# One scheduler flag: the queues of a two-block attention kernel laid by a timeline simulation

## The chip, the cores and the metric

The kernel runs on one core of one Trainium2 chip. The metric is the device time of one execution in microseconds (us). TensorE (PE) multiplies, VectorE (DVE), ScalarE (ACT) and GpSimd (POOL) work elementwise, and SyncE (SP) issues most of the loads. Each engine takes its instructions from a queue of its own, strictly in the order in which they stand there, and waits where an operand or a buffer is not ready.

## What is computed

Two transformer blocks run one after the other on 512 tokens of width 1024, everything in float32. Cut to what matters:

```
mod = silu(c) @ w_ada + b_ada                       # shift, scale, gate
h   = rms_norm(x, g_pre) * (1 + scale) + shift
proj = h @ w_in                                     # qa ka va fa za | qb kb vb zb
oa  = forgetting_attention(qa, ka, va, fa) * silu(za)    # "fox": 8 heads of 64, causal, with decay
ob  = sliding_window_sink_attention(rope(qb), rope(kb), vb) * silu(zb)   # "SWA": 8 query heads, 2 kv heads
x   = x + gate * rms_norm(concat(oa, ob) @ w_out, g_post)

h = rms_norm(x, norm_g);  mem_h = rms_norm(mem, mem_norm_g)
c_glu, c_gate, d_q, d_k, d_v, d_gate, x_q, x_gate, merge = split(h @ w_in_2)
y_conv = conformer_conv(c_glu, c_gate)              # a*sigmoid(b), depthwise convolution with 31 taps, layer norm, projection
y_diff = differential_attention(d_q, d_k, d_v)      # 8 heads, two softmax maps each, p0 - lam * p1, norm, projection
y_mem  = memory_cross_attention(x_q, mem_h)         # 4 heads of 256 over 256 memory tokens, projection
g = sigmoid(merge);  x = x + (g0*y_conv + g1*y_diff + g2*y_mem) @ w_out_2
```

## The kernel before

**Products.** Every float32 operand of a large product is split into a high and a low part; a product is three matmuls, hi·hi, hi·lo and lo·hi. A weight chunk is loaded as `raw` (load_w, the DMA at L164), ACT casts it to `wh` (L169), DVE or POOL subtracts to get `wl` (L171). mm_T (L190) streams 512 tokens per matmul, mm_N (L199) 256 columns. 128x128 transposes are PE instructions too (`tp`).

**Stages.** First come the loads, the memory's keys and values (their normalisation ends in L463 on `mk`) and the modulation: for each of eight chunks of w_ada a product of one row is summed on DVE as scale-and-add steps (gemv, L317 to L320), and its result makes one slice of the normalised input (ada, L366 to L373, `hh` and `hl`). Then the SWA items (scores at L655), then the fox items (scores L735 and L736, softmax L738 to L742, transposes and split causal_tp L751 to L754, values fox_pv L773), then w_out and the norms (finish, with hn at L817 and its transposes at L821), then the differential attention of the second block (scores L1022 and L1023, softmax L1025 to L1032, values L1056), the memory attention (scores L1157), and at the end the three branch projections, the merge and w_out_2. The gate row of the first block (gate_row) is eight more such one-row products, run as filler of the fox items. A tile's name with its number, as sc_3174, stands for one buffer of the program; it is the same tile before and after.

**What sets the order.** An attention stage is a list of items. For each item a helper emits the scores, the values of an earlier item, the transposes of the one before, and then pieces of other work out of a queue of generators (`fill`), a generator's piece being a group of matmuls:

```
    def staged(items, first, second, last, lag, k):
        for i in range(n + lag + 1):
            if i < n:
                first(items[i])
            if i - lag - 1 >= 0:
                last(items[i - lag - 1])
            if 0 <= i - lag < n:
                second(items[i - lag])
            fill(k(i) if callable(k) else k)
```

For the fox items these are the projections that later heads need (qk2, qk3), the gate za1 and the gate row, and after the last item the split of the eight head pairs for w_out, of which the first two take the buffers of the first values:

```
    staged([(pr, m, n) for pr in range(4) for m in range(2) for n in range(NT)], fox_sc, fox_tp, fox_pv, 2, 1)
    o45 = [fa.tile([P, 2, S], F32R, tag=t, name="o45") for t in ("vh0", "vl0")]
```

So no w_out matmul can stand ahead of the last matmul that reads vh0 and vl0 (pv_3395, head pair 1). The convolution's 30 taps per channel tile (L904, after the first at L902) are emitted with a low priority, so that DVE takes them where it has nothing else. All of this is only the order of emission and its priorities: the tile framework then walks through a simulated execution of the program and puts, engine by engine, the ready instruction of the highest priority next into that engine's queue. The queues are fixed before anything runs on the chip.

## Time and profile before

| what | value |
|---|---|
| three runs | 1195.54, 1196.16 and 1196.78 us, median 1196.16 |
| the profiled execution | 1196.61 us, of which the span of the trace is 1194.8 |
| TensorE's mean granted clock in it | 0.991 of full speed |
| busy: PE, DVE, ACT, POOL | 1154.0, 926.6, 551.7, 213.3 us |
| chain of waits that ended last | PE 63%, DVE 24%, issue 3%, ACT 1% of the span |
| moved by DMA | 165.43 MB, 138 GB/s |

"Busy" of PE counts each matmul from its start to a modelled end, and since matmuls are pipelined these overlap: 24 matmuls of 512 columns, each listed with about 0.39 us, start within 5.5 us. What PE has to do is therefore better counted from start to start. A stage below is named by the first score matmul of the item with which it begins; the first start of these on PE is at 131.6 us (sc_1686, the first SWA item), 209.1 (sc_2589, the first fox item), 253.5 (sc_3174), 291.5 (sc_3593), 304.3 (sc_3737, the last fox item), 410.6 (sc_5129, the first differential item), 701.2 (sc_8482, the last), 745.2 (sc_8881, memory attention) and 827.0 (sc_9755).

### The profile page before, as it was taken

Reading aid. Unit: us, or ns where it says so; the run is one execution under the profiler, and the core shown is the slowest. Engines: PE = TensorE matmul, PEld = TensorE weight load, DVE = VectorE, ACT = ScalarE, POOL = GpSimd, SP = SyncE. Lnnn points to the kernel's source line nnn. Section 1 sums busy time; section 2 is a strip of 40 time slices with the busy share of each in tenths; the row PEclk is TensorE's granted clock in tenths of the full one; section 3 lists DMA queues with packets and bytes.
Section 4 is the critical chain, followed back from the end, with each engine's and each line's share of the span. In section 5 each row is a group of like instructions: output and inputs, shape, how many; then the busy total and the mean of one; then the engine's idle time right before and its main releaser. Section 6 shows DMA issues by size and latency. Waiting matters only on the chain.

```text
span 1194.8 us, 18995 instructions
## 1 busy us (share of the span) xinstructions
PE 1154.0 (97%) x6960; PEld 1015.9 (85%) x6960; DVE 926.6 (78%) x2055; ACT 551.7 (46%) x1173; POOL 213.3 (18%) x161
## 2 busy tenths in 40 slices
PE   7879999999989999999999999999999999999998
PEld 6878887878889988998999887988888888888898
DVE  6997777898686699999989999999692596543341
ACT  7646566557554354445554452544422354232230
POOL 1334200000112211120111221221010132011020
PEclk9989999999999999999999999999999999999999
DMA  8765312443463423324233343333446755433232
GB/s 336 259 212 164 105 56 87 152 148 110 150 231 131 124 71 98 106 89 115 89 116 106 124 141 106 106 116 106 152 147 227 267 186 185 132 97 101 86 123 79
DMA packets 61965, 165.43 MB, mean 138 GB/s; under 512 B 7120, under 2 KB 15568, under 8 KB 60848
## 3 DMA queue, kind: packets, MB, share of 16 engines
q1 hardware_dynamic: 36560, 122.41, 32.5%
q10 hardware_dynamic: 25312, 41.82, 10.0%
q8 instruction: 55, 0.90, 0.3%
q14 instruction: 38, 0.31, 0.1%
HBM read 136.80 MB, written 20.58 MB: 132 GB/s over the span
## 4 chain that ended last, share of the span: by engine, by line
PE 63%; DVE 24%; issue 3%; ACT 1%; DMA 0%; POOL 0%; ACTq 0%; DVEq 0%; POOLq 0%
PE mm L190 40%; PE mm L199 15%; DVE cv L904 7%; DVE wl L171 3%; DVE dp L1025 1%; PE pv L773 1%; DVE dp L1032 1%; PE tp L751 1%; DVE dp L1031 1%; DVE ptl L754 1%; PE sc L1157 1%; PE pv L694 1%; PE pv L1200 1%; DVE qs L259 1%; PE tp L266 1%
## 5 line engine op out<-in xcount | busy, mean ns | idle before, releaser
L169 ACT CAST wh<-raw 128x512 fp32r<-128x512 f32 x372 | 215.3, 620 | 217.7 <-PE mm L190 96.2
L171 POOL TENSOR_TENSOR wl<-raw,wh 128x512 fp32r<-128x512 f32 (+1 forms) x93 | 141.8, 1525 | 831.9 <-ACT wh L169 668.8
L171 DVE TENSOR_TENSOR wl<-raw,wh 128x512 fp32r<-128x512 f32 (+1 forms) x279 | 201.7, 747 | 95.3 <-ACT wh L169 94.9
L190 PE MATMUL mm<-hh,wh 128*128 128x512 f32 x640 | 255.9, 400 | 0.0
L190 PE MATMUL mm<-hh,wl 128*128 128x512 f32 x640 | 251.8, 393 | 0.0
L190 PE MATMUL mm<-hl,wh 128*128 128x512 f32 x640 | 251.7, 393 | 0.0
L199 PE MATMUL mm<-wh,hh 128*128 128x256 f32 (+1 forms) x672 | 193.5, 289 | 0.2 <-ACT hh L824 0.2
L904 DVE SCALAR_TENSOR_TENSOR cv<-u,vec,cv 128x512 f32<-128x512 f32 x240 | 191.1, 796 | 3.4
L199 PE MATMUL mm<-wl,hh 128*128 128x256 f32 (+1 forms) x672 | 190.7, 284 | 0.3 <-POOL wl L171 0.3
L199 PE MATMUL mm<-wh,hl 128*128 128x256 f32 (+1 forms) x672 | 190.8, 284 | 0.0
L190 PEld LDWEIGHTS mm<-hh,wl 128*128 128x128 f32 x640 | 120.5, 188 | 27.0
L190 PEld LDWEIGHTS mm<-hh,wh 128*128 128x128 f32 x640 | 120.6, 188 | 24.7
L190 PEld LDWEIGHTS mm<-hl,wh 128*128 128x128 f32 x640 | 120.8, 189 | 24.5
L199 PEld LDWEIGHTS mm<-wl,hh 128*128 128x128 f32 x672 | 128.5, 191 | 0.8 <-POOL wl L171 0.6
L199 PEld LDWEIGHTS mm<-wh,hh 128*128 128x128 f32 x672 | 127.9, 191 | 0.8 <-ACT hh L824 0.5
L199 PEld LDWEIGHTS mm<-wh,hl 128*128 128x128 f32 x672 | 128.3, 191 | 0.0
L190 PE MATMUL mm<-bh,wh 128*128 128x512 f32 x192 | 75.9, 396 | 0.0
L190 PE MATMUL mm<-bh,wl 128*128 128x512 f32 x192 | 75.4, 393 | 0.0
L190 PE MATMUL mm<-bl,wh 128*128 128x512 f32 x192 | 75.4, 393 | 0.0
L1027 ACT ACTIVATE dp<-dp,dst 128x128 f32<-128x128 f32 (+3 forms) x64 | 35.5, 556 | 54.8 <-DVE dst L1025 54.6
L199 PE MATMUL mm<-wl,mh 128*128 128x256 f32 x128 | 39.3, 307 | 6.5 <-DVE wl L171 6.5
L190 PEld LDWEIGHTS mm<-bl,wh 128*128 128x128 f32 x192 | 36.1, 188 | 8.4 <-issue 0.2
(326 smaller groups left out, 2122.4 us busy)
## 6 DMA issues: line engine op xcount, KB each, us to landing
raw<-in_w_dram SPq DMA_DIRECT2D x120, 512.0 KB
raw<-in_w_out_dram SPq DMA_DIRECT2D x24, 512.0 KB
raw<-in_w_mem_dram SPq DMA_DIRECT2D x16, 512.0 KB
ada<-in_w_ada_dram SPq DMA_DIRECT2D x8, 1024.0 KB
ada<-in_w_gate_dram SPq DMA_DIRECT2D x8, 512.0 KB
k<-ks SPq DMA_DIRECT2D x32, 128.0 KB
o_d<-sph ACTq DMA_DIRECT2D x16, 256.0 KB
o_d<-spl ACTq DMA_DIRECT2D x16, 256.0 KB
```

Source lines behind the costliest of these rows:

```text
L169: act.copy(out=wh[:, s], in_=raw[:, s])
L171: eng.tensor_tensor(out=wl[:, s], in0=raw[:, s], in1=f(wh[:, s]), op=ALU.subtract)
L190: m = pe.matmul(out=ps, lhsT=a[:, c0:c0 + P], rhs=at(b, k), start=(n == 0 and i == 0), stop=(n == KT - 1 and i == 2))
L199: pe.matmul(out=ps, lhsT=at(a, k)[:, t * P:(t + 1) * P], rhs=b[:, 0:n], start=(start and m == 0 and i == 0), stop=(stop and m == len(order ...
L259: dve.scalar_tensor_tensor(out=s[b], in0=ps[a], scalar=sc, in1=f(s[a]), op0=ALU.mult, op1=ALU.subtract)
L266: pe.transpose(out=ps[:, t * P:(t + 1) * P], in_=src[:, t, c0:c0 + P], identity=ident)
L694: pe.matmul(out=pv4[0:64], lhsT=l_, rhs=r_[:, j], start=(cnt == 0), stop=(cnt == 3 * nk - 1))
L751: pe.transpose(out=tp[:, j * P:(j + 1) * P], in_=pt_[:, j * P:(j + 1) * P], identity=ident)
L754: dve.tensor_tensor(out=ptl[:, 0:n + 1, n * P:w], in0=tv, in1=f(pth[:, 0:n + 1, n * P:w]), op=ALU.subtract)
L773: pe.matmul(out=pv[0:64, j * P:], lhsT=l_, rhs=r_[:, j, j * P:], start=(j == 0 and i == 0), stop=(j == NT - 1 and i == 2))
L904: dve.scalar_tensor_tensor(out=a, in0=u[:, j:j + S], scalar=dw[:, m * 31 + j:m * 31 + j + 1], in1=a, op0=ALU.mult, op1=ALU.add)
L1027: act.activation(out=p_[:, :w], in_=p_[:, :w], func=AF.Exp, scale=-1.0, bias=st_[:, 0, n, m:m + 1], accum_out=st_[:, 1, n, m:m + 1])
```

## The change

The tile context is told to lay the queues with another simulation of the program, one that takes its times from a timeline model; emission order, priorities, tiles, transfers and arithmetic stay.

```
-    with tile.TileContext(nc) as tc:
+    with tile.TileContext(nc, schedule_with_timeline_sim=True) as tc:
```

Each engine has the same instructions on the same tiles before and after, also the same number of them; only their order in the queues differs. PE's matmuls stand on average 14 places from where they were (at most 124), DVE's instructions 9, ACT's 5, POOL's and SP's about 1. From sc_9755 on, the order is practically that of before.

**First place: PE among the fox items.** The score matmuls of two successive items (L735, L736; sc_3506, sc_3534), before:

```order
L735 MATMUL sc_3506<-k1_3291,qs_3254 128x256
L736 MATMUL sc_3506<-k2_3293,q2_3292 128x256
L751 MATMUL tp_3514<-cst_79,fp_3434 128x128 x4
L190 MATMUL mm_3521<-hh_83,wh_3446 128x512
L190 MATMUL mm_3521<-hl_84,wh_3446 128x512
L190 MATMUL mm_3521<-hh_83,wl_3447 128x512
...
L735 MATMUL sc_3534<-k1_3291,qs_3254 128x384
L736 MATMUL sc_3534<-k2_3293,q2_3292 128x384
```

and now:

```order
L735 MATMUL sc_3474<-k1_3291,qs_3254 128x128
L736 MATMUL sc_3474<-k2_3293,q2_3292 128x128
L751 MATMUL tp_3412<-cst_79,fp_3333 128x128
L735 MATMUL sc_3506<-k1_3291,qs_3254 128x256
L736 MATMUL sc_3506<-k2_3293,q2_3292 128x256
L773 MATMUL pv_3395<-pth_3149,vh_2028 64x512
L735 MATMUL sc_3534<-k1_3291,qs_3254 128x384
L736 MATMUL sc_3534<-k2_3293,q2_3292 128x384
```

Before, twelve projection matmuls (mm_3521, L190) stand between two items. In the new order the last of them stand ahead of sc_3330, six items earlier, and between these items there is nothing but the attention itself. From sc_1686 to sc_3174 there are now 325 matmuls of L190 where there were 224, and from sc_3174 to sc_3593 11 where there were 112.

**Second place: DVE at the last of the eight products for the modulation** (acc_985, whose sum L320 the last slice of hh waits for), before:

```order
L319 SCALAR_TENSOR_TENSOR acc_985<-ada_890,cs_106,acc_985 128x256
L319 SCALAR_TENSOR_TENSOR acc_986<-ada_890,cs_106,acc_986 128x256
L171 TENSOR_TENSOR wl_1128<-raw_1125,wh_1127 128x528
L368 SCALAR_TENSOR_TENSOR mod_188<-sc_976,vec_78 128x2
L320 TENSOR_TENSOR acc_985<-acc_985,acc_986 128x256
```

and now:

```order
L317 TENSOR_SCALAR acc_985<-ada_890,cs_106 128x256
L319 SCALAR_TENSOR_TENSOR acc_986<-ada_890,cs_106,acc_986 128x256
L320 TENSOR_TENSOR acc_965<-acc_965,acc_966 128x256
L369 SCALAR_TENSOR_TENSOR gs_187<-mod_188,vec_78 128x1
L171 TENSOR_TENSOR wl_1314<-raw_1311,wh_1313 128x512
L319 SCALAR_TENSOR_TENSOR acc_985<-ada_890,cs_106,acc_985 128x256
L171 TENSOR_TENSOR wl_1314<-raw_1311,wh_1313 128x512
```

Ahead of the last L320 DVE now has 30 subtractions of L171 where it had 25, and all eight L463, of which it had none there. On SP two chunks of the first projection's weights (w1c) and one of the next stand ahead of the fourth pair of memory weights and of the second pair of x loads (L379, which wait for a buffer).

**Third place: DVE among the differential items** (softmax of the second item of a head: L1025 takes scores and row maximum, L1029 to L1032 normalise; L904 are taps, L210 to L219 a reciprocal root in ten small steps), before:

```order
L217 TENSOR_SCALAR ru_5411<-rt_5410 128x32
L1029 RECIPROCAL drr_5085<-dst_5084 128x2
L904 SCALAR_TENSOR_TENSOR cv_5023<-u_5020,vec_78,cv_5023 128x512
L218 TENSOR_TENSOR rt_5410<-rt_5410,ru_5411 128x32
L1030 TENSOR_TENSOR drr_5085<-drr_5085,nlam_104 128x1
L904 SCALAR_TENSOR_TENSOR cv_5023<-u_5020,vec_78,cv_5023 128x512
L219 SCALAR_TENSOR_TENSOR ry_5409<-rt_5410,ry_5409 128x32
L1031 TENSOR_SCALAR dp_5478<-dp_5478,drr_5085 128x128
```

and now:

```order
L211 TENSOR_SCALAR ry_5409<-rv_5408 128x32
L1029 RECIPROCAL drr_5085<-dst_5084 128x2
L171 TENSOR_TENSOR wl_5739<-raw_5736,wh_5738 128x512
L904 SCALAR_TENSOR_TENSOR cv_5023<-u_5020,vec_78,cv_5023 128x512
L171 TENSOR_TENSOR wl_5739<-raw_5736,wh_5738 128x512
L212 TENSOR_TENSOR rt_5410<-ry_5409 128x32
L1030 TENSOR_TENSOR drr_5085<-drr_5085,nlam_104 128x1
L904 SCALAR_TENSOR_TENSOR cv_5023<-u_5020,vec_78,cv_5023 128x512
```

The small steps of the reciprocal root are spread over a longer stretch and the weight subtractions stand earlier. On PE the transposes of an item (L751) and its values (L1056) now stand behind 10 to 20 matmuls of projections that followed them before.

## Rows read from the trace of the kernel before

**Rows 1.** The page's first part: busy us, share of the span, instructions.
```profile
PE 1154.0 (97%) x6960; PEld 1015.9 (85%) x6960; DVE 926.6 (78%) x2055; ACT 551.7 (46%) x1173; POOL 213.3 (18%) x161
```

**Rows 2.** The chain that ended last, in time order: start, us, what.
```profile
283.91 2.75 PE mm L190 x12
...
417.43 5.75 PE mm L199 x48
...
978.40 166.59 PE mm L190 x720
1144.99 45.96 PE mm L199 x384
```

**Rows 3.** Stages: us; busy PE, PEld, DVE, ACT, POOL (instructions); clock; DMA share, GB/s.
```profile
131.60:209.10 77.50, 76.53 (x459) 64.42 (x459) 60.26 (x187) 49.67 (x136) 9.69 (x12) 1.00 0.23 69
209.10:253.50 44.40, 43.64 (x271) 37.38 (x269) 39.74 (x134) 23.19 (x59) 3.88 (x3) 1.00 0.53 162
253.50:291.50 38.00, 37.41 (x193) 30.24 (x193) 34.36 (x102) 23.23 (x55) 2.82 (x2) 1.00 0.41 125
291.50:304.30 12.80, 12.38 (x92) 11.00 (x91) 12.19 (x40) 10.40 (x27) 1.30 (x1) 1.00 0.18 45
304.30:410.60 106.30, 101.57 (x788) 96.70 (x787) 73.89 (x148) 53.52 (x107) 22.41 (x18) 1.00 0.52 167
410.60:701.20 290.60, 283.23 (x1901) 259.48 (x1901) 281.05 (x691) 140.48 (x318) 49.14 (x29) 1.00 0.34 102
701.20:733.10 31.90, 31.24 (x155) 25.90 (x153) 31.69 (x58) 12.74 (x26) 8.22 (x5) 1.00 0.44 148
733.10:745.20 12.10, 9.57 (x44) 8.11 (x44) 10.85 (x21) 2.71 (x8) 0.00 (x0) 0.86 0.27 91
745.20:827.00 81.80, 81.68 (x506) 72.62 (x505) 76.00 (x133) 39.89 (x84) 18.13 (x12) 1.00 0.33 107
827.00:1194.80 367.80, 363.93 (x1779) 305.06 (x1777) 199.06 (x286) 114.58 (x206) 54.53 (x35) 1.00 0.45 148
```

**Rows 4.** The same view in stretches of 4 us.
```profile
68.00:72.00 4.00, 2.00 (x9) 1.74 (x10) 4.00 (x11) 3.12 (x6) 2.00 (x1) 0.59 0.86 333
72.00:76.00 4.00, 2.22 (x11) 1.93 (x10) 3.90 (x9) 1.80 (x3) 1.55 (x2) 0.50 0.93 367
340.00:344.00 4.00, 2.43 (x22) 2.23 (x21) 3.72 (x10) 3.33 (x8) 1.28 (x1) 1.00 0.98 309
```

**Rows 5.** DVE's groups at 209.1 to 304.3: busy us, mean ns | idle before.
```profile
L319 DVE SCALAR_TENSOR_TENSOR acc<-ada,cs,acc 128x128 f32<-128x128 f32 x48 | 16.5, 377 | 0.0
L738 DVE CUSTOM_DVE_ANT_0 fp<-sc,cst 128x128 f32<-128x128 f32 (+3 forms) x30 | 14.1, 474 | 2.8 <-PE sc L736 2.5
L742 DVE TENSOR_SCALAR fp<-fp,fst 128x128 f32<-128x128 f32 (+3 forms) x29 | 12.7, 439 | 0.3
L754 DVE TENSOR_TENSOR ptl<-tp,pth 128x128 fp32r<-128x128 f32 (+3 forms) x27 | 12.7, 473 | 0.4 <-ACT pth L753 0.3
L800 DVE TENSOR_TENSOR ohl<-oz,ohl 128x512 fp32r<-128x512 f32 x4 | 2.8, 706 | 2.0 <-PE sc L735 2.0
```

**Rows 6.** DVE's groups at 40 to 92.3 us.
```profile
L171 DVE TENSOR_TENSOR wl<-raw,wh 128x512 fp32r<-128x512 f32 (+1 forms) x15 | 11.9, 825 | 0.0
L463 DVE TENSOR_SCALAR mk<-mk,ry 128x256 f32<-128x256 f32 x8 | 3.4, 474 | 0.0
```

**Rows 7.** DVE's timeline at the last L320: start, us; in brackets idle before.
```profile
81.93 0.16 DVE L368 SCALAR_TENSOR_TENSOR mod<-sc,vec 128x2 f32<-128x2 f32 x1 [1.97 <-PE sc L367]
82.01 0.41 DVE L320 TENSOR_TENSOR acc<-acc 128x256 f32<-128x256 f32 x1
```

**Rows 8.** PE's waits, whole run: us in total, times, longest us.
```profile
PE tp L240 <- DVE xql L1138: 2.5, 1, 2.5
PE tp L821 <- DVE hn L817: 2.3, 2, 1.6
PE tp L240 <- DVE qs L259: 2.0, 3, 1.0
```

## The prediction

> **What bounds the kernel now.** I read the page's busy times first [rows 1]: PE is busy 97% of the span, DVE 78%. Those 97% flatter PE, because matmuls overlap. The chain that ended last shows what one really takes: 12 matmuls of 512 columns in 2.75 us, 0.229 each, and 48 of 256 columns in 5.75 us, 0.120 each [rows 2]. With these, and about 0.11 for 128 columns (the 256-column time bounds it), all matmuls come to about 1111 us of the span of 1194.8. So some 84 us of it are head and waits, and a change of order can only touch those. Next I read busy time by stage [rows 3]. After 827.0 PE is busy 363.93 of 367.8 us and the chain runs through single pieces of 167 and 46 us of matmuls: PE alone sets the end there, and any time lost or won ahead of it reaches the end in full. In the differential stage (410.6 to 701.2) DVE is busy 281.05 of 290.6 us, while the matmuls need 273.7: DVE is the tighter one. In the SWA and fox stages PE is ahead, DVE at 78% to 95%. Last I read PE's waits [rows 8]: they are short and few, two of 2.5 us at most.
>
> **The change part by part.** No instruction is added or removed, so each term is a difference in PE's waiting. I cut both orders at the same score tiles and counted what stands between.
>
> *Start, to 131.6.* Ahead of the last sum of the modulation, DVE gets five more L171 and eight L463: 5 x 0.825 + 8 x 0.474 = 7.9 us by their rows [rows 6]. Neighbours on DVE overlap: at 209.1 to 304.3 the groups sum to 102.6 us where DVE was busy 39.74 + 34.36 + 12.19 = 86.3 [rows 3], a factor of 0.84. So 6.6 us come ahead of the L320 that started at 82.0. DVE was idle 1.97 us just before it [rows 7], which absorbs as much, and PE has about 2 us less of its own left afterwards. On SP, the w1c loads go ahead of the x loads that block the queue, so products start earlier, but three weight chunks also go ahead of loads of the modulation. I take +2; bounds +6 (nothing absorbed) and -4 (the earlier loads win and the later DVE work was on the path).
>
> *SWA and fox, 131.6 to 304.3.* This is the largest term. From sc_1686 to sc_3174, 101 more L190 (23.1 us) and ten fewer small matmuls (1.2) stand in PE's queue: 138.0 us of matmuls instead of 116.1. Before, this stretch took 77.5 + 44.4 = 121.9 [rows 3], 5.8 more than its matmuls. With denser filling I expect about 3 of those to stay: 141.0. From sc_3174 to sc_3593 the bill comes: 11 fillers instead of 112, PE has 11.6 us of matmuls where it had 36.3 (in 38.0 us). The w_out matmuls can't help, since their first operand needs the buffers that pv_3395 reads. DVE has 13 L319, 8 L738, 9 L742, 8 L754 and 6 L800 there: 4.9 + 3.8 + 4.0 + 3.8 + 4.2 = 20.7 us [rows 5], and some 26 smaller ones with the reads of the row maxima about 8.5 by their own groups: 29.2, or 24.6 us with the factor 0.84. In the stretch nearest to this, where the items ran with few fillers (209.1 to 253.5), DVE was busy 39.74 of 44.4 [rows 3]; at that share 24.6 us take 27.5. PE then works under half of the time, and its clock matters. At 68 to 76 us PE was busy 2.0 and 2.2 of 4 us and was granted 0.59 and 0.50 of full speed, the lower level of 1.2 GHz; at 340 to 344 it was busy 2.43 of 4 and kept 1.00 [rows 4]. The new stretch, 11.6 of 27.5, is nearer to the first, so I add 1.5 for slower scores and transposes on the item's own chain: 29. The Trainium skill ("TensorE: Matmul & The Clock Gate", HAM oscillation) says that recurring idle gaps send the clock to the lower level and that full speed comes back only after sustained work; by that the whole stretch would run slow and this term would be about 3 us more, while the row at 340 speaks for less. From sc_3593 to sc_3737 PE gets 16.6 us of matmuls instead of 11.7 (12.8 us before): 17. Sum 141 + 29 + 17 = 187 against 121.9 + 38.0 + 12.8 = 172.7; the new order has done 2.1 us more of matmuls by then, so the net is **+12**. Lower bound +5: the two score buffers let PE run two items ahead of DVE, so the bare stretch costs it 23, and only 2 us are lost before it. Upper bound +20: 33 in the bare stretch at the lower clock, 6 lost before it as now, and 18 after.
>
> *w_out and norms, 304.3 to 410.6.* The transposes of the last hn (L821) stood behind 8 matmuls of the next product; now 73 stand ahead of them, 7.8 us of cover for a wait of 2.3 in all [rows 8]. Against that, the last fox values have fewer fillers beside them. I take -2; the stage has 106.3 - 101.57 = 4.7 us of PE idle in all [rows 3], so at best -4; at worst +1.5.
>
> *Differential stage.* At every score tile both orders have done the same PE work within 3 us and the same DVE work within 5. What moves is finer: transposes and values stand behind 10 to 20 matmuls, which covers the DVE steps that they wait for, and the small steps of the reciprocal root are spread between taps. DVE's idle time is 290.6 - 281.05 = 9.5 us [rows 3]; that is all that can be won, and I expect half: -5. At worst +2, if a transposition that comes later makes DVE wait at L754 in its turn.
>
> *Memory attention, 701.2 to 827.0.* PE needs 117.5 of 125.8 us; it loses 2.5 waiting for xql [rows 8] and runs at 0.86 clock at 733 to 745 [rows 3]. The new order has 10 us more of matmuls and 15 more of DVE ahead of sc_9009. If PE and DVE were tied closely there, 66 us of DVE and then 59 of PE would give 125, no gain; if loosely, all 8 could go. I take -4, bounds -8 and +3.
>
> *After 827.* The same order: 0.
>
> Sum: 2 + 12 - 2 - 5 - 4 = +3 on the profiled execution's 1196.61, so 1199.6. The median of the runs lies 0.45 below that execution; hence **1199 us**. From no change a measurement of this kernel can tell 0.2%, 2.4 us.
>
> **The rivals.**
> - *Faster.* The waits in the last stages go and the bare fox stretch is cheap: start 0, fox +6, norms -2, differential -7, memory -5, sum -8: **1188**. For it speaks that PE's waits of 17 and 8 us over its matmuls in those two stages are behind DVE steps of one item, just what the new order covers; against it that DVE is nearly full there. It decides where PE, two items ahead, loses less than 8 us between sc_3174 and sc_3593 and DVE's idle time in the differential stage falls below 3.
> - *Much slower.* The same fox mechanism at its dear end: the clock stays at the lower level through the bare stretch and each item's chain runs by itself. Fox +16, start +3, norms -2, differential -2, memory -1, sum +14: **1210**. Rows 4 at 68 to 76 speak for it, the row at 340 against.
> - *No change, 1196.* The waits only change places: what PE idles in the fox stretch (about +12) it saves later to the us. The terms cancel easily, so this is no far case.
> - That the flag does nothing is excluded: the queues differ.
>
> **How the numbers follow.** My forecast, slower by a few us, is the likeliest with 0.30; the dear end gets 0.17 (slower together 0.47), no change within 0.2% 0.19, faster 0.34. The bounds added up reach from 1176 to 1228, but they don't all fall one way; five terms with half-widths of 4 to 8 give about 11 either side, and to take in the middle of both outer rivals I go to 1184 and 1211.
>
> **What would show it.** Between sc_3174 and sc_3593 the new profile should show PE busy for under half of the time, a clock below 1.0 there, and waits for L738, L742 and L754 that the old one doesn't list; sc_1686 to sc_3174 should last about 141 us. DVE's idle time from sc_5129 to sc_8482 should be about 5 us instead of 9.5. The wait for hn should be gone, and sc_9755 to the end should again take 368 us. I am wrong if the bare stretch takes under 23 us or if sc_3737, which by the sum starts at 321, starts before 312; if sc_1686 starts more than 6 us away from 131.6, the start was misread.

## The result, and the profile after

The changed kernel takes 1208.83 us (median of 4 runs, 1208.32 to 1210.07); the kernel before took 1196.47 in the same session. The ratio is 1.0105 (95% interval 1.0088 to 1.0123): slower, by some 12 us. The profiled execution has a span of 1206.5 us against 1194.8, a granted clock of 0.986 against 0.991, and the same busy times within 0.5 us on PE, DVE, ACT and POOL. The engines do the same work, so the difference is waiting, and one stretch at a lower clock.

The changed kernel by stage, cut at the same score tiles as [rows 3] (length, then busy us of PE, PEld, DVE, ACT and POOL, granted clock, DMA):

```profile
133.40:213.60 80.20, 80.20 (x479) 69.48 (x478) 60.54 (x185) 49.26 (x134) 10.78 (x13) 1.00 0.24 73
213.60:274.30 60.70, 59.44 (x342) 50.37 (x341) 47.66 (x146) 31.07 (x75) 5.89 (x4) 1.00 0.53 154
274.30:302.20 27.90, 20.59 (x83) 15.22 (x82) 23.17 (x81) 13.84 (x34) 1.27 (x1) 0.69 0.34 104
302.20:322.20 20.00, 17.69 (x130) 15.47 (x129) 16.08 (x51) 12.01 (x33) 1.29 (x1) 1.00 0.18 53
322.20:428.90 106.70, 100.05 (x764) 95.08 (x765) 71.96 (x149) 53.95 (x109) 21.85 (x17) 0.98 0.47 154
428.90:714.50 285.60, 281.31 (x1891) 258.27 (x1890) 279.33 (x675) 140.33 (x317) 51.16 (x29) 1.00 0.35 104
714.50:838.80 124.30, 121.47 (x712) 106.50 (x712) 119.06 (x225) 55.54 (x117) 26.46 (x17) 1.00 0.36 116
838.80:1206.50 367.70, 363.84 (x1779) 305.05 (x1778) 199.39 (x287) 114.69 (x206) 53.73 (x35) 1.00 0.45 148
```

The first fox half (from sc_2589 to sc_3174) went from 44.4 to 60.7 us, the stretch after it from 38.0 to 27.9, the last part from 12.8 to 20.0. The two late stages shrank, 290.6 to 285.6 and 125.8 to 124.3. After sc_9755 the time is 367.7 as before (367.8).

In the fox stage the sum of DVE's work is the same, 87 us here and 86 before, but DVE idles 21.7 us in it instead of 8.9. In the first half it is 60.7 - 47.66 = 13.0 us, of which 6.7 are two waits for the last SWA values and 2.5 are waits for loads of the gate row. The two longest stand at its beginning (DVE's timeline: start, us; in brackets the idle time before and what ended it):

```profile
216.42 0.43 DVE L700 SCALAR_TENSOR_TENSOR oz<-oz,stm 128x256 f32<-128x256 f32 x1 [2.39 <-ACT stm L698]
...
223.89 0.43 DVE L700 SCALAR_TENSOR_TENSOR oz<-oz,stm 128x256 f32<-128x256 f32 x1 [4.26 <-ACT stm L698]
```

L700 needs the values of the last SWA items, whose matmuls stand among and behind projections in PE's queue. PE is full there. Fifty microseconds later it is the other way round: DVE has 23.17 of 27.9 us to do and PE, out of projections, waits for it. PE's waits behind the start (engine, line, what for: us in all, times, longest), of which only the one for hn was among the longer ones before [rows 8]:

```profile
PE pv L773 <- ACT pth L753: 2.9, 2, 2.2
...
PE sc L735 <- DVE fst L738: 2.4, 5, 0.8
PE mm L199 <- ACT ohl L799: 2.0, 1, 2.0
PE pv L773 <- DVE ptl L754: 1.9, 3, 1.4
PE tp L717 <- DVE acc L320: 1.8, 1, 1.8
PE tp L821 <- DVE hn L817: 1.8, 1, 1.8
PE mm L199 <- DVE o L800: 1.7, 1, 1.7
```

The changed kernel in stretches of 4 us: the clock falls to its lower level in the bare stretch, and PE is part idle once more at the last fox values, inside what is counted as the norms' stage:

```profile
274.30:278.30 4.00, 3.96 (x22) 3.15 (x20) 3.90 (x13) 2.94 (x7) 0.00 (x0) 1.00 0.61 167
...
282.30:286.30 4.00, 2.57 (x8) 1.59 (x9) 3.97 (x14) 1.70 (x5) 0.00 (x0) 0.50 0.58 163
...
294.30:298.30 4.00, 3.93 (x15) 2.98 (x15) 3.84 (x15) 2.79 (x8) 0.00 (x0) 0.50 0.00 0
...
330.30:334.30 4.00, 2.66 (x16) 1.66 (x15) 1.25 (x2) 1.41 (x3) 0.00 (x0) 1.00 0.00 0
334.30:338.30 4.00, 2.34 (x12) 2.34 (x13) 1.38 (x2) 1.26 (x3) 0.00 (x0) 0.74 0.68 209
```

### The profile page after: what moved, and what is told of

Same layout as the page of the kernel before. It is cut to its first block, busy times and chain, and to the rows that moved or that the text cites. A ratio compares the mean times of both kernels' runs of the same rounds, so it can differ in the third digit from the quotient of the medians.

```text
span 1206.5 us, 19005 instructions
## 1 busy us (share of the span) xinstructions
PE 1153.6 (96%) x6960; PEld 1018.2 (84%) x6960; DVE 926.9 (77%) x2055; ACT 552.0 (46%) x1173; POOL 213.6 (18%) x161
## 4 chain that ended last, share of the span: by engine, by line
PE 78%; DVE 14%; DMA 3%; issue 2%; ACT 1%; POOL 0%; SPq 0%; ACTq 0%; POOLq 0%; DVEq 0%
PE mm L190 42%; PE mm L199 25%; DVE cv L904 4%; DVE wl L171 2%; PE pv L773 1%; PE tp L751 1%; PE tp L266 1%; PE pv L694 1%; DVE acc L319 1%; PE pv L1056 1%; DMA ada<-in_w_gate_dram 1%; PE sc L1022 1%; PE sc L1023 1%; PE pv L1200 1%; DMA klz<-v_d 1%
## 5 line engine op out<-in xcount | busy, mean ns | idle before, releaser
L169 ACT CAST wh<-raw 128x512 fp32r<-128x512 f32 x372 | 212.1, 620 | 216.3 <-PE mm L190 100.4
L171 POOL TENSOR_TENSOR wl<-raw,wh 128x512 fp32r<-128x512 f32 (+1 forms) x93 | 143.6, 1544 | 843.5 <-ACT wh L169 733.1
L171 DVE TENSOR_TENSOR wl<-raw,wh 128x512 fp32r<-128x512 f32 (+1 forms) x279 | 204.9, 754 | 91.6 <-ACT wh L169 86.4
L190 PE MATMUL mm<-hh,wh 128*128 128x512 f32 x640 | 253.3, 396 | 0.0
L190 PE MATMUL mm<-hl,wh 128*128 128x512 f32 x640 | 252.9, 395 | 0.0
L190 PE MATMUL mm<-hh,wl 128*128 128x512 f32 x640 | 252.4, 394 | 0.0
L904 DVE SCALAR_TENSOR_TENSOR cv<-u,vec,cv 128x512 f32<-128x512 f32 x240 | 197.6, 823 | 2.1
L190 PEld LDWEIGHTS mm<-hh,wl 128*128 128x128 f32 x640 | 120.4, 188 | 25.5
L190 PEld LDWEIGHTS mm<-hl,wh 128*128 128x128 f32 x640 | 120.5, 188 | 24.9
L190 PEld LDWEIGHTS mm<-hh,wh 128*128 128x128 f32 x640 | 120.4, 188 | 24.6
L190 PE MATMUL mm<-bh,wh 128*128 128x512 f32 x192 | 75.9, 396 | 0.0
L190 PE MATMUL mm<-bh,wl 128*128 128x512 f32 x192 | 75.4, 393 | 0.0
L190 PE MATMUL mm<-bl,wh 128*128 128x512 f32 x192 | 75.4, 393 | 0.0
L319 DVE SCALAR_TENSOR_TENSOR acc<-ada,cs,acc 128x256 f32<-128x256 f32 (+1 forms) x96 | 44.7, 487 | 0.2
L190 PEld LDWEIGHTS mm<-bh,wh 128*128 128x128 f32 x192 | 36.1, 188 | 8.4 <-issue 0.2
```

The source lines that it names most:

```text
L169: act.copy(out=wh[:, s], in_=raw[:, s])
L171: eng.tensor_tensor(out=wl[:, s], in0=raw[:, s], in1=f(wh[:, s]), op=ALU.subtract)
L190: m = pe.matmul(out=ps, lhsT=a[:, c0:c0 + P], rhs=at(b, k), start=(n == 0 and i == 0), stop=(n == KT - 1 and i == 2))
L319: dve.scalar_tensor_tensor(out=d[k % 2], in0=a[:, k, :], scalar=cs[:, k:k + 1], in1=d[k % 2], op0=ALU.mult, op1=ALU.add)
L904: dve.scalar_tensor_tensor(out=a, in0=u[:, j:j + S], scalar=dw[:, m * 31 + j:m * 31 + j + 1], in1=a, op0=ALU.mult, op1=ALU.add)
```

## The experiments

Below, a stage's loss is its length less its matmuls counted from start to start (0.2285 us for 512 columns, 0.1193 for 256, 0.1087 for 128), all cut at the same items. Before, the SWA and fox items lose 8.5 us, the norms 7.0, the differential stage 16.9, the memory attention 8.4; in the changed kernel 22.7, 9.9, 12.7 and 6.1. The start (to sc_1686) varies between 131.2 and 133.4 us over runs that have the old queues there, and between 133.3 and 136.5 over runs with the changed kernel's (136.5 in run 9, whose queues are the same to the last instruction), so differences of 3 us in it mean nothing. The ratios below are against runs of the kernel before on the same chip (medians 1194.95 to 1196.86).

**1 and 2. Hold the fillers back.** With the flag, each filler matmul gets an order-only dependency on the score matmul of the item after which it is emitted; once for SWA and fox, once for fox alone.

```
 m = pe.matmul(out=ps, lhsT=a[:, c0:c0 + P], rhs=at(b, k), ...)        # mm_T, and the same in mm_N
+if hold[0] is not None:
+    after(m, hold[0])
...
-        pe.matmul(out=ps[:, :w], lhsT=q2[:, n * P:w], rhs=k2[:, :w], start=False, stop=True)
+        hold[0] = pe.matmul(out=ps[:, :w], lhsT=q2[:, n * P:w], rhs=k2[:, :w], start=False, stop=True)
```

> Timeline scheduler, and every filler matmul of the SWA and fox items held (in PE's queue alone) behind the score matmul of the item after which it is emitted. Theory A (the fillers run ahead and leave the late fox items and the last fox values bare): sc_1686 to sc_3737 takes 172 to 177 us instead of 188.8, w_out and norms 103 to 105 instead of 106.7, the stages after it as in the changed kernel (285.6 and 124.3), so the total is 1188 to 1195, below the kernel before. Theory B (the new order of DVE, ACT and SP in the fox stage, with the gate row's products and their loads, is what stalls): that stretch still takes over 183 us and the total is 1203 or more.

> As the run before, but only the fox items hold their fillers; the SWA items use up theirs early and the last three SWA items stand bare. Theory A: the bare stretch only moves, from fox to the end of SWA, and is shorter there (few items): 3 to 8 us more than with both held, 1193 to 1201. Theory B: no better than the changed kernel, 1203 to 1210.

Measured 1209.43 us (ratio 1.0107, 1.009 to 1.0125) and 1207.88 (1.01, 1.0083 to 1.0118): theory A missed the total, and theory B's figures held (sc_1686 to sc_3737 takes 188.0 us in the first run, over its 183). The bare stretch did go, its loss falls from 16.3 to 6.7 and 3.8 us. But the first fox half now loses 11.6 and 12.6 where it had lost 2.5, and SWA and fox together still lose 21.3 and 20.1. The first run's windows, first and second part of the fox stage:

```profile
206.90:255.70 48.80, 42.61 (x249) 35.18 (x247) 38.03 (x127) 24.80 (x65) 4.28 (x3) 0.93 0.45 136
255.70:323.70 68.00, 62.73 (x346) 52.36 (x346) 53.44 (x161) 35.50 (x83) 5.42 (x4) 0.97 0.38 113
```

DVE idles 10.8 and 14.6 us in these; a part of it, 5.3 us, is the first line, and PE's longest waits are the two below it:

```profile
DVE acc L322 <- DMA ada<-in_w_gate_dram: 5.3, 5, 2.5
...
PE sc L742 <- DVE fst L745: 4.4, 5, 2.5
PE sc L742 <- DMA k<-k: 4.2, 1, 4.2
```

So theory B had something: with the fillers held, DVE stalls on data that come late. But these runs do not put a mended PE queue beside the changed kernel's other queues: the simulation laid all of them anew around the hold. In the first run DVE's instructions of SWA and fox stand on average 7 places from the changed kernel's order and 5 from the old one (counted in the queues that the kernels give). Whether DVE's order alone would cost as much is not shown.

**3. The fillers early under the old scheduler.**

```
-        staged([...], swa_sc, swa_tp, swa_pv, 1, 2)
+        staged([...], swa_sc, swa_tp, swa_pv, 1, 3)
...
-    staged([...], fox_sc, fox_tp, fox_pv, 2, 1)
+    staged([...], fox_sc, fox_tp, fox_pv, 2, 2)
```

> The kernel before with its old scheduler, but three filler pieces per SWA item instead of two and two per fox item instead of one, so that the fillers are used up by about the twentieth fox item. Theory A: the bare stretch appears under the old scheduler too, with the clock below 0.8 there, and the total is 8 to 14 us above the kernel before: 1204 to 1210. Theory B: within 3 us of before, 1193 to 1199.

Measured 1207.23 us (1.009, 1.0073 to 1.0107), the total that theory A gave. SWA and fox lose 21.6 us. The same two parts as in the changed kernel, without the flag: DVE idle while PE runs projections, then PE idle. They weigh differently, though: sc_3174 to sc_3593 is short here (the last line) and its clock 0.88, not below 0.8 as expected, so most of the loss stands ahead of it.

```profile
276.00:280.00 4.00, 4.00 (x22) 3.39 (x21) 1.81 (x4) 2.29 (x5) 1.28 (x1) 1.00 0.77 275
280.00:284.00 4.00, 4.00 (x19) 3.28 (x18) 1.80 (x4) 1.07 (x3) 0.00 (x0) 1.00 0.39 135
...
289.80:303.80 14.00, 10.11 (x57) 7.60 (x55) 11.68 (x38) 11.97 (x30) 1.27 (x1) 0.88 0.25 68
```

**4. Transposes behind the fillers in the differential stage, old scheduler.**

```
+            if early:
+                fill(k(i) if callable(k) else k)
             if 0 <= i - lag < n:
                 second(items[i - lag])
-            fill(k(i) if callable(k) else k)
+            if not early:
+                fill(k(i) if callable(k) else k)
```

> The kernel before with its old scheduler; in the differential stage alone the fillers are emitted ahead of an item's transposes instead of behind them, so that some 24 projection matmuls stand between scores and transposes. Theory C (the changed kernel's 5 us gain there comes from transposes and values standing behind fillers on PE): the stage takes 285 to 288 us instead of 290.6, total 1191 to 1194. Theory D (it comes from DVE's order, taps and root steps interleaved): the stage stays at 290 to 292 or longer, total 1195 to 1199.

Measured 1219.18 us (1.0189, 1.0168 to 1.0209), worse than both theories allowed. The stage takes 313.6 us. Between the transposes of a head's last item and the values that need them there now stand 4 to 11 matmuls, where 24 to 52 stood before:

```profile
PE pv L1059 <- DVE ptl L757: 8.9, 4, 6.0
PE pv L1059 <- ACT pth L756: 6.9, 4, 3.0
```

Cover for one wait was taken from the next one.

**5 to 8. Queues written out.** The old scheduler, with order-only dependencies that fix the queue of chosen engines for a chosen stretch to that of one of the two kernels. Run 5 fixes every engine. In the others the engines that are not named are laid anew by the scheduler around the fixed one, so those runs are not exchanges of one queue with the rest held. (Instructions go through a recording wrapper, so in these kernels nearly every line reads L107.)

```
+        for q in ORDER:                 # one engine's instructions in the wanted order
...
+            for a, b in zip(q, q[1:]):
+                tc.add_manual_dep(INS[b], a, nosync, reason="issue order")
```

> Every engine's queue written out: up to the first differential score (sc_5129) in the order of the kernel before, from there in the order of the changed kernel. Theory A (each stage's gain or loss belongs to that stage's order): all up to 410.6 as before, then 286 us for the differential stage and about 124 for the memory attention, total 1188 to 1192, faster than both kernels. Rival E (the changed kernel gained there only because its loads had run further ahead during the losses before): 290 and 126 us again, total 1195 to 1198.

Measured 1191.28 us, ratio 0.9964 (0.995 to 0.9978): **faster than both kernels**, as theory A said. The differential stage takes 286.6 us by the same cuts, the memory attention 124.3; the fox stage's length is that of before:

```profile
211.00:306.20 95.20, 93.43 (x553) 78.54 (x552) 86.24 (x275) 56.85 (x140) 7.99 (x6) 1.00 0.44 131
412.00:698.70 286.70, 282.17 (x1892) 258.63 (x1891) 280.40 (x675) 140.44 (x317) 49.43 (x29) 1.00 0.34 104
698.70:823.00 124.30, 121.48 (x713) 106.49 (x712) 118.87 (x225) 55.54 (x117) 26.09 (x17) 1.00 0.36 117
```

So the late gain belongs to the late order, and does not live on what was lost earlier.

> Old scheduler, only SP's queue up to sc_5129 in the changed kernel's order (w_gate loads later, behind weight chunks that wait for a buffer); the other engines as the old scheduler then lays them. Theory F (PE's order makes the loss in the fox stage): 1195 to 1199. Theory G (late w_gate loads hold up DVE and with it the items): SWA to last fox item loses over 14 us instead of 8.5, total 1201 to 1209.

Measured 1220.27 us (1.0204, 1.0187 to 1.0221), beyond theory G's range. All of it lies between sc_3174 and sc_3593, which takes 61.6 us instead of 38.1. PE's longest wait in it, and then DVE's:

```profile
PE tp L107 <- DVE acc L107: 16.4, 5, 12.9
```

```profile
DVE acc L107 <- DMA ada<-in_w_gate_dram: 11.7, 4, 7.7
```

The gate row's products stand early in DVE's and PE's queues as laid here, and their loads come late: SP issues the last of the eight at 292.6 us instead of 256.9. PE stands still at a transposition of the gate row, with the items behind it.

> Old scheduler, only PE's queue up to sc_5129 in the changed kernel's order; the other engines as the old scheduler then lays them around it. Theory F: sc_1686 to sc_3737 takes 184 to 192 us as in the changed kernel (188.8), the norms 106 to 107, total 1206 to 1213. Theory H (it is DVE's order, steps that stand ahead of their data): under 180 us and a total of 1196 to 1202.

Measured 1232.23 us (1.0311, 1.0292 to 1.033), again beyond the range. The fox part is as theory F said: sc_1686 to sc_3737 takes 191.9 us and loses 25.8. This does not rule out theory H, since DVE's order came along: laid around PE's new order, it stands on average 2 places from the changed kernel's and 9 from the old one. The rest is elsewhere, 9 us more lost in the start and 8 in the norms, where the other engines were laid around a PE order not their own.

> Timeline scheduler, only PE's queue up to sc_5129 in the order of the kernel before; the other engines as the timeline scheduler then lays them. Theory F: sc_1686 to sc_3737 takes 172 to 177 us, later stages keep their gain, total 1188 to 1196. Theories G and H: DVE still stalls on w_gate loads or on PE, over 182 us, total 1201 to 1210.

Measured 1216.35 us (1.0175, 1.016 to 1.0191). sc_1686 to sc_3737 takes 181.9 us, just under the bound that I gave for G and H: with PE's old order 5 of the 14 us are won back (the loss is 17.7 instead of 22.7). It is not that the other queues stayed the flag's: DVE's stands here on average 3 places from the old order and 10 from the changed kernel's. What makes the rest of the loss, with PE's order the old one and DVE's near it, stays open. The start loses 9 us more, the norms 2.5 more than in the changed kernel, and the total lies above what any of the theories gave.

**9. What the clock costs.** All queues as in the changed kernel, and in the bare stretch each item's first score matmul four times more:

```
+        for _ in range(EXTRA if pr == 2 else 0):          # EXTRA = 4
+            n0 = nc.tensor.matmul(out=ps[:, :w], lhsT=q1[:, n * P:w], rhs=k1[:, :w], start=True, stop=True)
...
         pe.matmul(out=ps[:, :w], lhsT=q1[:, n * P:w], rhs=k1[:, :w], start=True, stop=False)
```

> Every queue written out in the changed kernel's order; in addition the first score matmul of the eight items from sc_3330 to sc_3593 is issued four more times ahead of the real one (its result is overwritten), 32 matmuls, 5.1 us at the full clock, in the stretch that stands bare of fillers. Theory K (the lowered clock is a large part of the 16.3 us lost there): the added work keeps the clock at 0.9 or above, the stretch takes 24 to 28 us instead of 27.9 although PE has 5 us more to do, and the total is 1203 to 1208. Rival L (DVE and the items' chain set the stretch, the clock costs little): it takes 28 to 33 us and the total is 1208 to 1214.

Measured 1209.35 us (1.0112, 1.0093 to 1.0132). The stretch:

```profile
277.50:304.60 27.10, 21.08 (x115) 16.49 (x114) 23.55 (x83) 14.36 (x35) 1.27 (x1) 0.94 0.33 103
```

Neither theory fits whole. The clock is back at 0.94 instead of 0.69 and the stretch is 0.8 us shorter with 5.1 us more on PE, inside K's range; but the total is that of the changed kernel, as L said. The total says little here: in the profiled execution the start alone is 3.1 us longer than in the changed kernel, with the same queues. DVE was busy 23.17 us in the stretch, and shorter than that it can't be while DVE has this work in it. So the clock's price lies between 0.8 us and 27.9 - 23.2 = 4.7. The changed kernel's chain that ended last narrows it: two groups of values stand in it at the low clock (the first two lines), and a like one after the stretch at full clock (the third).

```profile
284.57 3.05 PE pv L773 x11
...
298.03 2.77 PE pv L773 x11
...
313.88 1.53 PE pv L773 x11
```

An estimate from these rows is 3.05 + 2.77 - 2 x 1.53 = 2.8 us. In these pieces PE does set the pace, and DVE's longest wait in the stretch, 3.1 us for a transposition, stands right behind the second.

**10. SP's old order with the flag.**

> Timeline scheduler, only SP's queue up to sc_5129 in the order of the kernel before (w_gate loads about 15 to 28 us earlier); the other engines as the timeline scheduler then lays them. Theory G (late w_gate loads are a part of the loss): sc_1686 to sc_3737 falls from 188.8 to 184 us or less, total 1200 to 1205. Theory F (PE's early fillers make it): 187 to 190 us, total 1206 to 1211.

Measured 1208.89 us (1.0117, 1.0098 to 1.0137), in F's range; sc_1686 to sc_3737 takes 192.3 us, over F's too, and none of it is won. But this run does not decide against G, since the loads did not come earlier: counted from sc_1686 the eight are issued at 91 to 152 us here and at 93 to 152 in the changed kernel. DVE waits for them 7.5 us here. What speaks against the late loads as the main cause is the changed kernel's own trace, in which DVE waits for them 2.5 us in all, and run 8, which issues them at 79 to 131 us and still loses 17.7.

**11 and 12. The differential stage, one engine fixed at a time, old scheduler.**

> Old scheduler, only DVE's queue from sc_5129 to sc_8482 in the changed kernel's order, the others as the old scheduler then lays them. Theory D (the gain in the differential stage comes from DVE's order): 285 to 288 us instead of 290.6, total 1191 to 1194. Theory C (from PE's): 290 us or more, total 1195 to 1200.

> Old scheduler, only PE's queue from sc_5129 to sc_8482 in the changed kernel's order, the others as the old scheduler then lays them. Theory C: 285 to 288 us instead of 290.6, total 1191 to 1194. Theory D: 290 us or more, total 1195 to 1200. If neither this run nor the one before gains, the gain needs both orders together.

Measured 1214.6 us (1.0149, 1.013 to 1.0169) and 1203.24 (1.0068, 1.0048 to 1.0087). The stage takes 306.6 and 300.5 us instead of 290.6, DVE being busy as much as ever (windows of the eleventh and the twelfth):

```profile
411.30:717.90 306.60, 288.59 (x1902) 260.76 (x1901) 279.50 (x687) 142.76 (x318) 46.47 (x29) 0.99 0.32 97
```

```profile
409.10:709.60 300.50, 287.87 (x1902) 263.83 (x1901) 283.80 (x677) 141.38 (x319) 48.46 (x30) 0.98 0.32 99
```

Each alone, with the others laid anew around it, loses 10 to 16 us; all the new queues together (run 5) win 4. Neither C nor D is borne out, but the runs are no clean halves: in the eleventh PE's queue moved on average 8 places from the old one, so that only 4 to 33 matmuls stand between a head's last transposes and its values (24 to 52 before), and in the twelfth DVE's moved 6. That the new orders gain together is shown; which part of them would gain in the old queues as they were is not.

## Why the prediction was right

The sign, the place and roughly the size of the main term held; the total was 10 us short of the measured one. The measured time lies nearest to the dear rival (1210, given 0.17), though not by that rival's terms, which had fox at +16 and the norms won. It is inside the range, but near its upper end (1211). The larger misses all fall to one side: 2.1 us in SWA and fox, 4.5 in the norms, 2.5 in the memory attention. By its own steps, on the profiled spans:

| step | foretold | measured |
|---|---|---|
| start, to sc_1686 | +2 | +1.9 (not clear of its variation) |
| SWA and fox, net of 2.1 us of matmuls done ahead | +12 | 188.9 - 172.7 - 2.1 = +14.1 |
| w_out and norms, with those 2.1 us given back | -2 | 106.7 - 106.3 + 2.1 = +2.5 |
| differential stage | -5 | 285.6 - 290.6 = -5.0 |
| memory attention | -4 | 124.3 - 125.8 = -1.5 |
| after sc_9755 | 0 | -0.1 |

- **Start.** The +2 came out by luck. The wait for the modulation's sums did grow, from 1.9 to 3.4 us, but the larger changes are two that the prediction did not have: the short waits for weights went and one long wait for the normalised x came. The prediction's "two of 2.5 us at most" [rows 8] had passed over the waits of the start. PE's longest there before:

```profile
PE mm L199 <- DVE wl L171: 6.6, 7, 1.8
PE mm L350 <- DMA mt<-in_mem_dram: 5.8, 2, 5.5
PE sc L367 <- DVE acc L320: 1.9, 2, 1.6
```

and now:

```profile
PE mm L391 <- DVE xn L386: 9.7, 1, 9.7
PE mm L350 <- DMA mt<-in_mem_dram: 5.7, 2, 5.3
PE sc L367 <- DVE acc L320: 3.4, 2, 3.2
```

- **SWA and fox.** sc_1686 to sc_3174 was to last 141 us and lasted 140.9. The bare stretch was put at 29 and took 27.9; sc_3593 to sc_3737 at 17 and took 20.0, which with the 1.1 us saved before it is the 2 us that this term is short: the w_out matmuls there waited 1.7 us for their own operand (o, L800). sc_3737 was to start at 321 and started at 322. Run 3 made a loss of the same size with the old scheduler, so fillers that run ahead are enough for it. That they are all of it is not borne out by runs 1, 2 and 8: with the fillers held or PE's old order, 17.7 to 21.3 us are still lost, in queues laid anew around it. What the prediction lacked was the other half: DVE, busy 86.3 of 95.2 us before, can't make up what it idles while PE runs ahead (21.7 us instead of 8.9). That its own new order is bound to PE's fits these runs, but no run has DVE's new order with the other queues as they were.
- **The clock.** It fell as foretold, 0.69 in the stretch; 1.5 us was allowed for it; run 9 puts it between 0.8 and 4.7, the rows of the chain near 2.8. The Trainium skill's rule on recurring gaps ("TensorE: Matmul & The Clock Gate", HAM oscillation) agrees with the fall of the clock, though the stretch was not slow as a whole: 0.69 is its mean, and its first row shows 1.00. The 4.5 us in all that the prediction worked out by it are at the end of what run 9 leaves room for. Of the signs that were named, PE's share of the stretch is under half only when its matmuls are counted from start to start at full clock (27.9 - 16.3 = 11.6 us); by busy time it is 20.59 of 27.9. A wait for L742 does not show.
- **Norms: the step that failed.** "73 stand ahead of them, 7.8 us of cover for a wait of 2.3" took one wait away, but 1.8 us of waiting for hn stayed, and the last fox values stood bare longer than the +1.5 at worst allowed: PE was half idle around 334 and waited 2.0 for ohl. This isn't the price of the bare stretch before it, since run 3, which has one too, loses 6.9 in the norms as before, and runs 1 and 2 with their fillers held lose 10.8 and 11.5: it belongs to the flag's order of this stage.
- **Differential stage.** DVE's idle time was to fall from 9.5 to about 5 and fell to 6.3; the term was right to the decimal, with some luck. The two reasons for it (transposes behind fillers, root steps between taps) are not shown one by one: runs 4, 11 and 12, which force either under the old scheduler and move other instructions with it, lost 10 to 23 us.
- **Memory attention.** Mis-sized: the two-step sum in the prediction, 125 us for close coupling, came nearer (124.3) than the -4 that was taken.

## What to carry to other kernels

Where two engines are both nearly full (here 90 and 86 of 95 us), count what each has to do between the same two marks in both orders: here a stretch in which one got its work early was paid for by the other's idling, and neither got it back. A set of queues is one solution; one engine's order forced on another set, with the rest laid anew around it, never gained here (six trials, 0 to 37 us slower than the set it came into), so compare and mix whole sets, stage by stage, at marks where both orders have done the same work. Mixed that way, the old order up to the differential stage and the new one from there, the kernel beat both (0.9964).

## What the runs showed of the hardware that was not expected

With SP's order changed and the other queues laid around it (run 6), eight loads of the gate row were issued 14 to 36 us later, and their stretch took 23.5 us more: a queue that waits holds up everything behind it, PE for 12.9 us at one transposition. And a TensorE at 0.69 of its clock for 28 us cost 4.7 us at most (run 9), and by the chain's rows about 2.8, since DVE, busy 23.17 of the 28 us, sets the pace in most of it.
